# Delta-rule layer of a four-layer decoder trunk: another order of the projection strips, GpSimd splits of the values' weights dropped, and the inverses' matmuls queued behind the third strip of values

## The chip, the cores and the metric

The kernel runs on one core of a Trainium2 chip. The metric is device time in microseconds of one execution. Before the change three runs took 872.19 (median), 870.34 and 872.74 us.

## The reference, cut to what matters

The trunk is four residual layers on 256 tokens of 1024 channels in float32: pooling mixer, gated delta rule, latent attention, pooling mixer again, then a last RMSNorm. The change is in the second layer, the gated delta rule. Of one head (8 heads, keys of 128, values of 256), with `q`, `k`, `v` from a projection, a causal convolution of four taps and SiLU:

```
proj = h @ w_in                                  # 1024 -> q 1024, k 1024, v 2048, gate 2048, b 8, a 8
A    = I + strict_lower((beta k) k^T * decay)    # per chunk of tokens
u, w = A^-1 (beta v),  A^-1 (beta k exp(g))      # a triangular solve
v_new  = u - w state
o      = (q exp(g)) state + lower(q k^T * decay) v_new
state  = state exp(g_last) + (k exp(g_last - g))^T v_new
y = (rmsnorm(o) * silu(gate)) @ w_out            # and x = x + y
```

The reference solves in chunks of 64 tokens; the kernel takes chunks of 128, so there are two chunks (16 triangles of 128 x 128 with the 8 heads) and one step of the recurrence.

## The kernel before, in words

**Split products.** Each float32 weight is split into two float32r parts, `hi` (a ScalarE cast, L117) and `lo` (raw minus hi, L119). A product takes three matmuls: hi by hi, hi by lo, lo by hi. `weights` (L101) loads one unit of two channel tiles of 128 x 512 with one or more DMAs on SyncE's queue into a `raw` buffer, casts each tile on ScalarE and subtracts on VectorE, or on GpSimd where the tile's number is in the argument `pool`. The `raw` buffer is free for the next load once both subtractions have read it.

**Strips.** The layer's projection is done in twelve strips of 512 columns, eight channel tiles each, by `project` (L132). A strip of keys, queries or values is made channel-major: 8 x 4 x 3 = 96 matmuls of 256 columns on L127 to L129 into two PSUM banks of `acc`; then come the convolution (ScalarE L633, VectorE L636), SiLU, transposes on TensorE (keys and queries L675, values L778) and, for values, a scaled copy on ScalarE (L781, tile `vR`). A strip of gates is token-major: 8 x 2 x 3 = 48 matmuls of 512 columns on L167, and two SiLUs on ScalarE (L556).

**The string `order` (L559)** lists the steps: g0 to g3 are gate strips, k and q strips of keys and queries, v0 to v3 values, d and a0, a1 the decays and the triangles (`LT`, L692), s the substitution, i the inverses, u0 and u1 the first chunk's new values.

```
order = "g0 k0 d a0 g1 k1 a1 s q0 v0 i v1 v2 q1 g2 u0 v3 u1 g3".split()   # L559
pool=((0, 4), (7,), (3, 7), (7,))[vi]        # gate, L553
pool=((1, 3, 5, 7), (3, 7), (), ())[vi]      # values, L767
```

**The substitution (s, L712)** inverts the 64 diagonal blocks of 32 x 32 at once, on 64 partitions of GpSimd. SyncE's queue writes the blocks out to DRAM (`d_l`, L718) and reads them back as `Lb` (L721); GpSimd then does 31 rounds of a product (L726, tile `pr`) and a subtraction (L730, tile `Tb`), each waiting for the one before; SyncE's queue writes `Tb` out (`d_t`, L732) and reads it into `T` in eight loads (L736).

**The inverses (i, L787)** grow these blocks to 64 and 128 by products on TensorE: `pairs` (L803, matmuls on L806 and L812) for both chunks, then `whole` (L817, L820, L824, L830). The first matmul of `pairs`, L806, reads `T`. The new values (u0, u1, L847) and all that follows read the inverses, `U`.

**What sets the order of the work.** The program is written in this order, but it is given to a planner (`schedule_with_timeline_sim=True`, L1236) that models the run beforehand and fixes for each engine, and for SyncE's DMA queue, one sequence of instructions. An instruction that is ready in the model goes ahead of those that stand earlier in the program and are not. On the chip each engine follows its sequence strictly: what the model placed early and what is late in fact holds up all that stands behind it on that engine. `later(...)` (L85) adds an order by hand: an instruction made within it comes after the named ones on the same engine. The planner also gives out buffers (`auto_bufs=True`).

Of the kernel before, what the change touches and what calls it, by code (L numbers as in the profile page):

```python
# [18 lines left out]
S = 256  # L19
# [23 lines left out]
def trunk(ctx: ExitStack, tc: tile.TileContext, x, positions, norm_g, pool_w_in, pool_w_grp,  # L43
# [24 lines left out]

# [1 line left out]
    def big(name, *dims, dt=F32):  # L70
# [14 lines left out]
    def later(*instructions):  # L85
        """What an engine gets within it comes after those of these that it gets too."""
        order = ExitStack()
        for ins in instructions:
            order.enter_context(tc.issue_after(ins))
        return order  # L90

    # weights that are ready early are not to be split ahead of a layer's input
    mark = {}
# [3 lines left out]
    def weights(src, n, cols, raw=None, pool=()):  # L97
        """One unit of weights, split into two float32r parts that add up to it."""
        if raw is None:
# [26 lines left out]
    def mm3(o, lhs, rhs, start, stop):  # L126
        nc.tensor.matmul(o, lhsT=lhs[0], rhs=rhs[0], start=start, stop=False)  # L127
        nc.tensor.matmul(o, lhsT=lhs[0], rhs=rhs[1], start=False, stop=False)  # L128
        nc.tensor.matmul(o, lhsT=lhs[1], rhs=rhs[0], start=False, stop=stop)  # L129

    def project(src, ks, act, cols=CW, chan=False, tail=0, done=None, cuts=1,
                where="acc", pool=()):  # L132
        """act (channel-major, split) times a block of columns; src(k0, n) is its weights.

        ks lists the units (first channel tile, how many), in the order to go through them.
        Token-major: one bank per token tile; channel-major: one bank per two
        channel tiles. The last `tail` units go by token tile and by `cuts` parts of the columns,
        each followed by done(t, part, its bank).
        """
        first, last = ks[0][0], sum(ks[-1]) - 1  # L140
# [5 lines left out]
        if chan:  # L146
            banks = [bank(acc if where == "acc" else aux, where) for _ in range(2)]
            for k0, n in ks:
                parts = unit(k0, n)
                for j in range(n):  # L150
                    k = k0 + j
                    for c in range(cols // P):
                        w = [v[:, c * P:(c + 1) * P] for v in parts[j]]
                        o = banks[c // 2][:, (c % 2) * S:(c % 2 + 1) * S]
                        mm3(o, w, act(k, 0, S), k == first and c % 2 == 0,
                            k == last and c % 2 == 1)
            return banks
# [33 lines left out]
    def split_out(*tiles):  # L191
        """Tiles of one bank, each (times a per-partition scale) into two float32r parts."""
        for ps, (hi, lo), scale in tiles:
# [17 lines left out]
    class Split:  # L211
        """Channel-major activations in two float32r parts, four channel tiles to a tile."""

# [18 lines left out]

    # ---- the residual stream. The square sum of a row but its last part goes along with that
    # part, as the square of one more column ----
    xs = [const.tile([P, D + 1], F32, name=f"x{t}") for t in range(NT)]
# [28 lines left out]
    make_identity(nc, ident)  # L264
    # the activation table and TensorE's clock, while the first loads run
    warm = small("warm", 2, bufs=1)
# [14 lines left out]
    class Normed:  # L281
        """The residual over its mean square's root, times a gain. Every other part of a row
        meets the gain before the root is known."""

# [27 lines left out]
    class LayerIn(Normed):  # L312
        """The normed residual of a layer, channel-major, made one token tile at a time."""

# [16 lines left out]
    def cols_of(w, c0, cols=CW):  # L331
        v = w.rearrange("(k p) c -> p k c", p=P)
        return lambda k0, n: v[:, k0:k0 + n, c0:c0 + cols]
# [14 lines left out]
    def layer_out(w, yT, ks, i):  # L348
        """The output projection into the residual, and the start of the next layer."""
        def done(t, a, ps):  # L350
# [20 lines left out]

# [1 line left out]
    place = {}  # L373
# [24 lines left out]
    def window_counts():  # L398
        """w / (t + 1) for the first tokens of the pooling windows."""
        cnt = workb("cnt", 16)  # L400
# [8 lines left out]

    # ================= multi-scale causal pooling =================  # L410
    def pool_layer(i, j, hT):
# [64 lines left out]
        for g in order:  # L476
            gs = gate(g)
            if not place:
                with later(*[m for k, m in mark.items() if k != "rest"]):
                    turn_params()  # L480
                    window_counts()
            elif setups:
                with later(*[m for k, m in mark.items() if k != "rest"]):
                    setups.pop(0)()
# [7 lines left out]

    # ================= gated DeltaNet =================
    GC = {}

    def gdn_setup():
# [15 lines left out]

        # convolution taps, one column per (tap, channel tile)
        crow = workb("crow", P)
# [20 lines left out]
    def gdn_layer(i, j, hT):  # L535
# [15 lines left out]
        def gate(vi):  # L551
            banks = project(cols_of(w_in, 2 * GDN_QK + GDN_V + vi * CW), units(KD), hT,
                            pool=((0, 4), (7,), (3, 7), (7,))[vi])  # L553
            gs.append(big("gsg", NT, CW))
# [3 lines left out]

        order = "g0 k0 d a0 g1 k1 a1 s q0 v0 i v1 v2 q1 g2 u0 v3 u1 g3".split()  # L559
        while order[0][0] == "g":  # L560
            gate(int(order.pop(0)[1]))

        # beta and the log decays
        ps = bank(aux, "aux")
# [36 lines left out]

        # decays: DT[t][j, h, i] = exp(G_i - G_j) for i >= j, and exp(G_i) for the second chunk
        ps = bank(aux, "aux")
# [24 lines left out]
        def conv(*tiles):  # L628
            """Causal depthwise convolution of the channel tiles of a bank."""
            def tp(n, c):  # L630
# [8 lines left out]

        # the substitution's unit diagonals, and room for the inverses  # L640
        Q, B = 4, 32
# [17 lines left out]
        def channels(dst, c0, hf, which):  # L659
            """Four heads of keys or queries, channel-major, and their square sums."""  # L660
            banks = project(cols_of(w_in, c0 + hf * CW), units(KD), hT, chan=True,
# [21 lines left out]
        def against(dst, rhs, sf, hf, t):  # L683
            """Keys against keys or queries of one chunk, decayed and scaled, four heads."""
            ps = bank(aux, "aux").rearrange("p (b s) -> p b s", b=4)
# [26 lines left out]
        def substitution():  # L712
            """Inverses of the unit lower triangles' 32 x 32 diagonal blocks; decayed keys."""
            d_l = dram.tile([M * Q, B * B], F32, name="d_l")
# [46 lines left out]

        # values, token-major, over the keys' inverse norms
        vR = []

        def values(vi):
            banks = project(cols_of(w_in, 2 * GDN_QK + vi * CW), units(KD), hT, chan=True,
                            pool=((1, 3, 5, 7), (3, 7), (), ())[vi])  # L767
            vR.append(big("vR", NT, CW))
# [18 lines left out]
        def inverses():  # L787
            """The blocks below the diagonal ones, by products: 32 to 64, 64 to 128.

            T is lower triangular and U its transpose. Of a product only the columns that  # L790
            the mask keeps are worked out: of two blocks of 32 each time, then of 64.
            """
            U.extend(big("U", H, P) for _ in range(NT))
# [40 lines left out]

            for stage in (pairs, whole):
                for t in range(NT):
                    stage(t)

        def news(hf):
            """The first chunk's new values."""  # L840
            h0 = 4 * hf
# [20 lines left out]

        # the two chunks, head by head
        yT = Split("yT", POOL_W // P)
# [9 lines left out]
        def unseen(h):  # L874
            """The second chunk's values less what the state holds for their keys."""
            ps = bank(aux, "aux")
# [57 lines left out]

    # ================= latent attention =================
    def rope_tables():
        """cos twice, and (-sin, sin), token-major."""
        inv = small("inv", HALF, bufs=1)
# [47 lines left out]
    def mla_layer(i, j, hT):  # L986
# [13 lines left out]
        def rotate(ps, t, nh, o):  # L1000
            """Rotary embedding of nh heads, token-major, from PSUM."""
            def shaped(a):
# [74 lines left out]

        # Products of 256 columns take split operands; the rest whole ones. Of queries and
        # probabilities that parts the token tiles.
        v, qT, kT, qrT = [], [], [], []  # L1080
# [73 lines left out]
        def flipped(h):  # L1154
            """Probabilities, key-major: the first keys for all queries, then the rest."""
            sb = probs.pop(h)
# [90 lines left out]
```

## Time and profile before

| | |
|---|---|
| median of three runs | 872.19 us |
| lowest and highest run | 870.34, 872.74 us |
| span of the profiled execution | 864.8 us |
| median less that span | 7.4 us |
| instructions | 16123 |
| HBM read, written | 137.79 MB, 1.58 MB |

The page of the profile tells of one execution. Its span runs from the first to the last instruction; what lies around it, about 7.4 us of the median, is not in the page. The page has each engine's busy time, then rows of 40 slices of the span (21.6 us each) in which a digit is a busy share in tenths, then the chain of work that ended last, then groups of instructions by line. The trace behind the page answers narrower questions: rows of one engine in order of time, who waited for whom, and busy time by stretch. A row of the timeline reads: start, duration, engine, line, operation, tile written <- tiles read, tile sizes, count, and in brackets the engine's idle time before it with what ended it. PE is TensorE's matmuls, PEld its weight loads, DVE VectorE, ACT ScalarE, POOL GpSimd, SPq SyncE's DMA queue.

The delta-rule layer runs from about 168 to 432 us of the span.

### The profile page before, as it was taken

Reading aid. Unit: us, or ns where it says so; the run is one execution under the profiler, and the core shown is the slowest. Engines: PE = TensorE matmul, PEld = TensorE weight load, DVE = VectorE, ACT = ScalarE, POOL = GpSimd, SP = SyncE. Lnnn points to the kernel's source line nnn. Section 1 sums busy time; section 2 is a strip of 40 time slices with the busy share of each in tenths; the row PEclk is TensorE's granted clock in tenths of the full one; section 3 lists DMA queues with packets and bytes.
Section 4 is the critical chain, followed back from the end, with each engine's and each line's share of the span. In section 5 each row is a group of like instructions: output and inputs, shape, how many; then the busy total and the mean of one; then the engine's idle time right before and its main releaser. Section 6 shows DMA issues by size and latency. Waiting matters only on the chain.

```text
span 864.8 us, 16123 instructions
## 1 busy us (share of the span) xinstructions
PE 843.5 (98%) x5965; PEld 779.9 (90%) x5965; DVE 590.0 (68%) x1138; ACT 488.1 (56%) x1007; POOL 156.6 (18%) x290
## 2 busy tenths in 40 slices
PE   7999999999999979999999999999999999999996
PEld 6999998988999868888989989988978989999986
DVE  5588776466889666466567658767766667867852
ACT  5566655468756535455555645555554566565542
POOL 4010000233258932022202002000000110000012
PEclk8999999999999989999999999999999999999999
DMA  6766656557565463123567676632542547566651
GB/s 211 235 194 185 183 172 219 171 158 228 158 172 168 124 191 102 46 84 137 146 183 221 170 171 194 190 104 75 171 146 59 181 144 207 188 180 191 196 194 50
DMA packets 111288, 140.43 MB, mean 162 GB/s; under 512 B 23340, under 2 KB 53224, under 8 KB 111208
## 3 DMA queue, kind: packets, MB, share of 16 engines
q1 hardware_dynamic: 109056, 138.17, 53.4%
q0 software_dynamic: 320, 1.06, 0.4%
q8 instruction: 47, 0.77, 0.4%
q10 hardware_dynamic: 1832, 0.16, 0.2%
q14 instruction: 33, 0.27, 0.1%
HBM read 137.79 MB, written 1.58 MB: 161 GB/s over the span
## 4 chain that ended last, share of the span: by engine, by line
PE 85%; POOL 7%; DVE 3%; DMA 2%; issue 1%; ACT 1%; SPq 1%; POOLq 0%; ACTq 0%; DVEq 0%
PE acc L167 34%; PE acc L128 11%; PE acc L127 11%; PE acc L129 11%; PE aux L127 2%; POOL Tb L730 2%; PE aux L128 2%; POOL pr L726 2%; PE aux L129 2%; DMA gain<-in_norm_g_dram 1%; PE aux L1134 1%; DVE h L303 1%; DVE wlo L119 1%; PE aux L688 1%; PE tp L1159 1%
## 5 line engine op out<-in xcount | busy, mean ns | idle before, releaser
L119 DVE TENSOR_TENSOR wlo<-raw,whi 128x512 fp32r<-128x512 f32 (+1 forms) x491 | 336.9, 709 | 166.6 <-ACT whi L117 160.1
L117 ACT CAST whi<-raw 128x512 fp32r<-128x512 f32 (+1 forms) x508 | 301.4, 617 | 262.8 <-PE acc L167 92.3
L127 PE MATMUL acc<-hTh,whi 128*128 128x256 f32 x832 | 235.8, 284 | 3.3 <-DVE cv L636 3.3
L128 PE MATMUL acc<-hTl,whi 128*128 128x256 f32 x832 | 236.1, 284 | 0.0
L129 PE MATMUL acc<-hTh,wlo 128*128 128x256 f32 x832 | 235.4, 283 | 0.0
L127 PEld LDWEIGHTS acc<-hTh,whi 128*128 128x128 f32 x832 | 158.2, 190 | 4.2 <-ACT whi L117 3.7
L128 PEld LDWEIGHTS acc<-hTl,whi 128*128 128x128 f32 x832 | 158.3, 190 | 0.4
L129 PEld LDWEIGHTS acc<-hTh,wlo 128*128 128x128 f32 x832 | 158.3, 190 | 0.2
L167 PE MATMUL acc<-whi,yTh 128*128 128x256 f32 (+1 forms) x384 | 116.3, 323 | 0.0
L167 PE MATMUL acc<-wlo,yTh 128*128 128x256 f32 (+1 forms) x384 | 116.2, 319 | 0.0
L167 PE MATMUL acc<-whi,yTl 128*128 128x256 f32 (+1 forms) x384 | 92.4, 321 | 0.0
L167 PEld LDWEIGHTS acc<-whi,yTh 128*128 128x128 f32 x384 | 71.9, 188 | 5.2
L167 PEld LDWEIGHTS acc<-wlo,yTh 128*128 128x128 f32 x384 | 72.0, 188 | 5.1
L167 PEld LDWEIGHTS acc<-whi,yTl 128*128 128x128 f32 x384 | 63.1, 188 | 5.6
L291 POOL TENSOR_TENSOR hg<-x,gain 128x256 f32<-128x256 f32 x18 | 15.4, 860 | 271.7 <-DVE x L353 267.9
L167 PE MATMUL acc<-wlo,hTh 128*128 128x512 f32 (+1 forms) x144 | 56.5, 396 | 0.8 <-DVE wlo L119 0.5
L167 PE MATMUL acc<-whi,hTh 128*128 128x512 f32 (+1 forms) x144 | 55.9, 394 | 0.7 <-ACT hTh L195 0.7
L167 PE MATMUL acc<-whi,hTl 128*128 128x512 f32 (+1 forms) x144 | 45.8, 390 | 0.0
L434 POOL COPY win<-u 128x4 f32<-128x4 f32 x8 | 2.8, 353 | 176.8 <-ACT u L428 176.8
L167 PEld LDWEIGHTS acc<-wlo,hTh 128*128 128x128 f32 x144 | 27.4, 191 | 7.6 <-DVE wlo L119 2.1
L167 PEld LDWEIGHTS acc<-whi,hTh 128*128 128x128 f32 x144 | 27.5, 191 | 6.6 <-ACT hTh L195 1.4
L119 POOL TENSOR_TENSOR wlo<-raw,whi 128x512 fp32r<-128x512 f32 x17 | 23.6, 1389 | 49.4 <-ACT whi L117 49.3
(336 smaller groups left out, 1440.8 us busy)
## 6 DMA issues: line engine op xcount, KB each, us to landing
raw<-in_pool_w_in_dram SPq DMA_DIRECT2D x60, 512.0 KB, 4.5
raw<-in_gdn_w_in_dram SPq DMA_DIRECT2D x48, 512.0 KB, 3.9
raw<-in_pool_w_out_dram SPq DMA_DIRECT2D x32, 512.0 KB, 3.9
raw<-in_mla_w_in_dram SPq DMA_DIRECT2D x24, 512.0 KB, 4.4
raw<-in_mla_w_uq_dram SPq DMA_DIRECT2D x36, 256.0 KB, 3.4
raw<-in_pool_w_grp_dram SPq DMA_DIRECT2D x16, 512.0 KB, 4.0
raw<-in_gdn_w_out_dram SPq DMA_DIRECT2D x16, 512.0 KB, 3.7
raw<-in_mla_w_ukv_dram SPq DMA_DIRECT2D x32, 256.0 KB, 3.2
```

Of the source, the lines that this page charges most:

```text
L117: a = nc.scalar.copy(hi, v)
L119: b = e.tensor_tensor(out=lo, in0=v, in1=hi.bitcast(F32), op=ALU.subtract)
L127: nc.tensor.matmul(o, lhsT=lhs[0], rhs=rhs[0], start=start, stop=False)
L128: nc.tensor.matmul(o, lhsT=lhs[0], rhs=rhs[1], start=False, stop=False)
L129: nc.tensor.matmul(o, lhsT=lhs[1], rhs=rhs[0], start=False, stop=stop)
L167: nc.tensor.matmul(o, lhsT=act(k, t * P, P)[x], rhs=parts[j][z][:, sl], start=k == first and x == z == 0, stop=k == last and x == 1)
L291: nc.gpsimd.tensor_tensor(out=self.early[t, a], in0=xs[t][:, sl], in1=self.g[:, sl], op=ALU.mult)
L303: nc.vector.scalar_tensor_tensor(out=h[:, cut:], in0=xs[t][:, sl], scalar=r[:, 0:1], in1=self.g[:, sl], op0=ALU.mult, op1=ALU.mult)
L688: nc.tensor.matmul(ps[:, b], lhsT=kT[hf][:, b, tt], rhs=rhs[hf][:, b, tt], start=True, stop=True)
L726: nc.gpsimd.tensor_tensor(out=pv, op=ALU.mult, in0=Lb[:, r, r + 1:, None].to_broadcast([M * Q, n, c]), in1=Tb[:, r:r + 1, :c].to_broadcast ...
L730: nc.gpsimd.tensor_tensor(out=tv, in0=tv, in1=pv, op=ALU.subtract)
L1134: nc.tensor.matmul(ps[:, spans[0]], lhsT=r0[bb, pr], rhs=krT[bb], start=False, stop=False)
```

## The change

Four things change; the rest of the diff takes out comments and docstrings.

```diff
@@ gate (L551)
-                            pool=((0, 4), (7,), (3, 7), (7,))[vi])
+                            pool=((0, 4), (7,), (), (7,))[vi])
...
-        order = "g0 k0 d a0 g1 k1 a1 s q0 v0 i v1 v2 q1 g2 u0 v3 u1 g3".split()
+        order = "g0 k0 d a0 g1 k1 a1 s q0 v0 g2 v1 v2 i q1 u0 v3 u1 g3".split()
@@ values (L765)
-            banks = project(cols_of(w_in, 2 * GDN_QK + vi * CW), units(KD), hT, chan=True,
-                            pool=((1, 3, 5, 7), (3, 7), (), ())[vi])
+            banks = project(cols_of(w_in, 2 * GDN_QK + vi * CW), units(KD), hT, chan=True)
@@ inverses (L787)
-            for stage in (pairs, whole):
-                for t in range(NT):
-                    stage(t)
+            with later(mark["pe"]):
+                for stage in (pairs, whole):
+                    for t in range(NT):
+                        stage(t)
@@ mm3 (L126), project (L155)
-        nc.tensor.matmul(o, lhsT=lhs[1], rhs=rhs[0], start=False, stop=stop)
+        return nc.tensor.matmul(o, lhsT=lhs[1], rhs=rhs[0], start=False, stop=stop).ins
...
-                        mm3(o, w, act(k, 0, S), k == first and c % 2 == 0,
-                            k == last and c % 2 == 1)
+                        mark["pe"] = mm3(o, w, act(k, 0, S), k == first and c % 2 == 0,
+                                         k == last and c % 2 == 1)
@@ pool_layer (L479, L483): the new mark is left out of what the setups come after
-                with later(*[m for k, m in mark.items() if k != "rest"]):
+                with later(*[m for k, m in mark.items() if k not in ("rest", "pe")]):
```

First, the third gate strip, g2, moves from behind the second strip of queries to a place ahead of the second strip of values, v1. Second, the inverses' step i moves from behind v0 to behind v2. Third, eight `lo` subtractions go from GpSimd to VectorE: four of v0, two of v1, two of g2. Fourth, the inverses' instructions on TensorE come, in TensorE's sequence, after the last channel-major matmul that stands ahead of them in the program, which is the last of v2. No arithmetic is added or removed.

More of the change, by code (lines that the diff above doesn't have):

```diff
@@ L482, in pool_layer @@
             elif setups:
-                with later(*[m for k, m in mark.items() if k != "rest"]):
+                with later(*[m for k, m in mark.items() if k not in ("rest", "pe")]):
                     setups.pop(0)()
```

## The prediction

> **What bounds the kernel now.** I read the page first, then TensorE in long stretches, then TensorE's waits and rows around the one stretch where it falls behind, then the engine behind that wait.
>
> ```profile
> span 864.8 us, 16123 instructions
> ...
> PE 843.5 (98%) x5965; PEld 779.9 (90%) x5965; DVE 590.0 (68%) x1138; ACT 488.1 (56%) x1007; POOL 156.6 (18%) x290
> ...
> PEclk8999999999999989999999999999999999999999
> ```
>
> TensorE is busy almost throughout, so a change that adds and removes no arithmetic can give back only time in which TensorE waits or is slow. After the start one slice of forty has a clock below full, the fifteenth (303 to 324 us), and it lies in the layer that changes. Busy time by stretch around it:
>
> ```profile
> 228.00:260.00 32.00, 31.62 (x270) 31.37 (x269) 26.81 (x57) 18.05 (x38) 14.13 (x10) 1.00 0.63 175
> 260.00:303.00 43.00, 43.00 (x319) 40.40 (x317) 35.10 (x72) 25.28 (x52) 39.25 (x57) 1.00 0.49 145
> 303.00:317.00 14.00, 8.13 (x43) 7.79 (x42) 8.72 (x16) 4.22 (x8) 7.23 (x13) 0.76 0.58 166
> 317.00:350.00 33.00, 32.96 (x253) 29.60 (x254) 21.49 (x36) 17.56 (x38) 5.31 (x6) 1.00 0.42 132
> ```
>
> The columns are the stretch, its length, the busy time of PE, PEld, DVE, ACT and POOL, the granted clock and DMA. TensorE is full up to 303 us and from 317 us on; between, it does 8.13 us of 14, at a mean clock of 0.76. The waits from 170 to 430 us, then TensorE's rows and the groups from 303 to 317 us:
>
> ```profile
> PE acc L127 <- DVE cv L636: 3.3, 1, 3.3
> PE aux L806 <- DMA T<-d_t: 2.6, 1, 2.6
> PE aux L830 <- DVE X L827: 0.8, 1, 0.8
> ```
>
> ```profile
> 302.54 0.63 PE L167 MATMUL acc<-whi,hTl 128*128 128x512 f32 x2
> 306.44 0.55 PE L127 MATMUL acc<-hTh,whi 128*128 128x256 f32 x1 [3.28 <-DVE cv L636]
> ...
> 312.72 0.28 PE L129 MATMUL acc<-hTh,wlo 128*128 128x256 f32 x1
> ...
> 313.43 0.28 PE L129 MATMUL acc<-hTh,wlo 128*128 128x256 f32 x1
> ...
> 314.13 0.28 PE L129 MATMUL acc<-hTh,wlo 128*128 128x256 f32 x1
> 317.04 1.97 PE L806 MATMUL aux<-T,LT 128*128 128x64 f32 x16 [2.63 <-DMA T<-d_t]
> ```
>
> ```profile
> L127 PE MATMUL acc<-hTh,whi 128*128 128x256 f32 x14 | 5.4, 386 | 3.3 <-DVE cv L636 3.3
> L128 PE MATMUL acc<-hTl,whi 128*128 128x256 f32 x14 | 5.2, 371 | 0.0
> L129 PE MATMUL acc<-hTh,wlo 128*128 128x256 f32 x14 | 5.1, 366 | 0.0
> ```
>
> So g2 ends at 303.17; TensorE waits 3.28 us for a bank that the convolution of q1 still holds; then 42 matmuls of v3 (14 + 14 + 14) take from 306.44 to 314.41, 7.97 us, the first of them slow; then it waits 2.63 us for `T`, and L806 starts the inverses at 317.04. At full clock six matmuls lie between 312.72 and 313.43, 0.118 us each, so the 42 are 4.96 us of work and the slow clock cost 3.0 us. The loss is 3.28 + 3.0 + 2.63 = 8.9 us. That is nearly all that a change of order can win in this stretch, 1.0% of the time.
>
> The next question is which of the three would still be there without the others. The chain of waits runs through GpSimd:
>
> ```profile
> 253.43 2.79 DMA d_l<-LT
> 256.33 3.82 DMA Lb<-d_l
> ...
> 310.87 2.94 DMA d_t<-Tb
> 314.76 2.19 DMA T<-d_t
> ```
>
> ```profile
> 260.22 0.23 POOL L726 TENSOR_TENSOR pr<-Lb,Tb 64x31 f32<-64x31 f32 x1 [1.51 <-DMA Lb<-d_l]
> ...
> 275.41 0.91 POOL L726 TENSOR_TENSOR pr<-Lb,Tb 64x231 f32<-64x231 f32 x1
> ...
> 293.80 1.28 POOL L119 TENSOR_TENSOR wlo<-raw,whi 128x512 fp32r<-128x512 f32 x1
> 295.04 0.58 POOL L726 TENSOR_TENSOR pr<-Lb,Tb 64x231 f32<-64x231 f32 x1
> ...
> 299.47 1.29 POOL L119 TENSOR_TENSOR wlo<-raw,whi 128x512 fp32r<-128x512 f32 x1
> 300.72 1.05 POOL L730 TENSOR_TENSOR Tb<-Tb,pr 64x192 f32<-64x192 f32 x1
> ...
> 310.60 0.25 POOL L730 TENSOR_TENSOR Tb<-Tb,pr 64x31 f32<-64x31 f32 x1
> ```
>
> The substitution runs from 260.22 to 310.85 us without a gap that matters, and with its two DMAs `T` reaches TensorE at 317.04. Had TensorE not waited at 303 us, it would only have come to L806 sooner and waited there. The substitution is the bound of this stretch. TensorE's end is therefore: when `T` arrives, plus all of TensorE's work that its sequence has put behind L806, since after 317 it is full.
>
> From 260.22 to 317.04 are 56.8 us, of which TensorE lost 8.9 and worked 47.9. The planner put L806 where it expected `T`, after 47.9 us of work; so in fact the chip's `T` came 8.9 us later than its plan.
>
> **The change part by part.** *GpSimd's splits.* Two of the eight lie inside the substitution, those of g2 at 293.80 and 299.47: 1.24 us up to 295.04 and 1.25 up to 300.72. Without them `T` comes 2.5 us sooner. The six of v0 and v1 lie ahead of it:
>
> ```profile
> L119 POOL TENSOR_TENSOR wlo<-raw,whi 128x512 fp32r<-128x512 f32 x6 | 9.1, 1510 | 14.3 <-ACT whi L117 14.3
> ```
>
> GpSimd waited 14.3 us among these six and 1.51 us more for `Lb`, so taking them away wins nothing. They go to VectorE:
>
> ```profile
> L119 DVE TENSOR_TENSOR wlo<-raw,whi 128x512 fp32r<-128x512 f32 (+1 forms) x491 | 336.9, 709 | 166.6 <-ACT whi L117 160.1
> ```
>
> At 0.709 us six are 4.3 us, in a stretch (228 to 260) in which VectorE is busy 26.81 of 32 us; it holds them, but `LT`, which the substitution's input waits for, is also made there. I take nothing for it, since a later start that the planner foresees lets TensorE do more ahead of it; unforeseen, up to 1.5 us, about two splits.
>
> *The splits do not leave the substitution alone on VectorE.* The product on 64x231 elements took 0.91 us at 275.41 and 0.58 at 295.04. VectorE's rows say what differs:
>
> ```profile
> L119 DVE TENSOR_TENSOR wlo<-raw,whi 128x512 fp32r<-128x512 f32 x27 | 22.1, 833 | 7.7 <-ACT whi L117 7.7
> ```
>
> ```profile
> 299.62 1.69 DVE L119 TENSOR_TENSOR wlo<-raw,whi 128x512 fp32r<-128x512 f32 x1 [7.04 <-ACT whi L117]
> ```
>
> From 292.6 to 299.6 VectorE stood still, and there the products run short; where it splits, they run 0.33 us longer. From 260 to 311 it made 27 splits. With g2's two it makes 29, and as it will not stand still for 7 us, up to four more: 0.7 to 2.0 us more for GpSimd. I take four splits, 1.3. So `T` moves by -2.5 + 1.3 = -1.2 us (-1.8 to -0.5), to 315.8.
>
> The Trainium skill, "SBUF — State Buffer", Terms, says that VectorE and GpSimd take turns at one shared port pair, and that the one that loses it stands still for the other's whole instruction. The trace agrees in direction (0.91 against 0.58); by that rule four splits of 0.709 us would take 2.8 us back, and the sum below would come out 1.5 us longer.
>
> *The stall on q1's convolution* (3.28 us and the slow clock behind it). Its cause is the load queue:
>
> ```profile
> SPq L104 <- POOL wlo L119: 28.8, 8, 8.6
> ```
>
> Loads waited up to 8.6 us for a `raw` buffer that a GpSimd split, queued behind the substitution, had not read; the 7.04 us of VectorE above are the same wait seen from its end, and q1's convolution was queued behind it. With the splits on VectorE and g2, which has no convolution, ahead of v1, this stall goes. What is late next is `T`: TensorE reaches L806 sooner and waits there. Alone this wins nothing.
>
> *The place of the inverses in TensorE's sequence.* Before the change L806 already stands behind v0, v1, v2, q1, g2 and 42 of 96 matmuls of v3. The strips ahead of it are the same set in the new order, so the order by hand behind v2 binds nothing. But the planner also counts on `T` coming earlier, by about the 2.5 us of the two splits; then L806 stands 2.5 us of work (21 matmuls) further ahead, and that work comes after `T`. That is +2.5 us (0 if the place does not move; a later place is the first rival).
>
> *The clock.* TensorE now has one wait instead of two: 56.8 - 1.2 - (47.9 - 2.5) = 10.2 us. Before, the slow 42 matmuls lay ahead of a wait for `T`, in its shadow; behind L806 nothing shadows them, and v3's matmuls, with which the inverses alternate, are full work. The nearest row is the stall of 3.28 us, whose aftermath cost 3.0; the wait of 2.63 cost nothing. A wait of 10.2 us is nearer the first, and I take 2.5 us (0 to 3.0).
>
> The Trainium skill, "TensorE: Matmul & The Clock Gate", Part 1, says that the array falls to half clock after an idle window of about 3.4 us and comes back after a busy one. The trace agrees (0.76 granted in 303 to 317 us); an estimate from that page is 1.7 to 3.4 us, which would leave the sum where it is.
>
> *The 0.8 us at L830* and the rest of the layer I leave as they are: their work and order do not change.
>
> Sum: -1.2 + 2.5 + 2.5 = +3.8 us: a span of 868.6 in place of 864.8. The median, 872.19, has 7.4 us beside that span; I move it by the same amount, to **876.0**. The ends: -1.8 + 0 + 0 = -1.8 (870.4), and -0.5 + 2.5 + 3.0 + 1.5 = +6.5 (878.7).
>
> **The rivals.** *First: the inverses fall later in TensorE's sequence (faster).* If all of v3 stands ahead of L806, its other 54 matmuls, 6.4 us, are done while `T` is on its way; TensorE gets there at 260.2 + 47.9 + 6.4 = 314.5, waits 1.3 us and keeps its clock: -1.2 - 6.4 = -7.6 us, 864.6. With part of g3 ahead too, the whole 8.9 us go: 863.3. It beats the forecast from the point at which some 20 matmuls more than before stand ahead. For it:
>
> ```profile
> 284.55 0.60 PE L778 MATMUL tp<-ident,vc 128*128 128x128 f32 x4
> ```
>
> ```profile
> 317.24 1.56 ACT L781 ACTIVATE vR<-tp,rki 128x256 f32<-128x256 f32 x4
> ```
>
> v1 was transposed by 285 us and copied out only at 317.24, beside the inverses' start: with i ahead of v1 in the program its tiles were granted behind the inverses'. With i behind v2 that knot is untied, and TensorE may run further before the planner's `T`. Against it: what places L806 is the substitution, and that gets shorter in the plan. Chance 0.28.
>
> *Second: the parts cancel (no change).* L806 keeps its place and the slow clock costs about 1.2 us: 0.0, 872.2. Chance 0.24.
>
> *Third: the order by hand does bind,* the planner expecting `T` so early that L806 stands right behind v2. Then q1 (96 matmuls) and 42 of v3, 138 x 0.118 = 16.3 us, come after `T`: -1.2 + 16.3 + 2.5 = +17.6, 889.8. Against it: before, it expected `T` a whole strip and a half later. Chance 0.07.
>
> *That the change does not do what it says* is so for the order by hand in my forecast already.
>
> **How the numbers follow.** The measurement tells about 0.3%, 2.6 us, from no change. My forecast, +3.8 us, has 0.41; with the third rival slower has 0.48, the same 0.24, faster 0.28. The forecast's own range is 870.4 to 878.7. For 8 in 10 it must reach to the first rival's 864.6: 864.0 to 879.0; left out are the third and the first's last microseconds.
>
> **What would show it.** Right: one wait of about 10 us of L806 for `T` with no stall on `cv` before it; fewer than 42 matmuls of v3 ahead of L806; no GpSimd row of L119 within the substitution, which ends about 1 us sooner after its start; a granted clock of one half just behind L806. Wrong: all of v3 ahead of L806 and no wait over 3 us (first rival), or L806 ahead of q1 (third). It is also wrong if TensorE is not full after L806, for then work moved behind it costs nothing.

## The result and the profile after

After the change twelve runs took 875.12 us (median; 872.12 to 877.44), twelve of the kernel before, beside them, 871.00 (868.08 to 872.74). The ratio is 1.0054 [1.0036, 1.0071]: slower by 4.1 us, with a forecast of +3.8. As will be seen, the sum came out right with some terms that were wrong.

The profiled execution of before, on which the prediction was built, was among its quickest. Over all executions the time is 1.7 us above the span, not 7.4, so that one took 866.6 us, 4.4 under the median, and its granted clock over the whole span was 0.991, where the mean of 87 runs of this kernel is 0.987.

The page of after:

```profile
span 872.5 us, 16110 instructions
...
PE 846.5 (97%) x5965; PEld 780.2 (89%) x5965; DVE 593.5 (68%) x1146; ACT 488.3 (56%) x1007; POOL 145.8 (17%) x282
...
PEclk9999999999999979999999999999999999999999
```

Eight instructions have left GpSimd (290 to 282) and eight have come to VectorE (1138 to 1146). The dip of the clock is in the fifteenth slice, as before, and deeper (7 for 8). TensorE's waits from 165 to 440 us:

```profile
PE aux L805 <- DMA T<-d_t: 7.0, 1, 7.0
PE acc L127 <- DVE vc L636: 1.6, 1, 1.6
PE aux L829 <- DVE X L826: 0.8, 1, 0.8
```

L805 is before's L806. The 3.3 us for `cv` are gone and the wait for `T` has grown from 2.6 to 7.0 us. The same stretches as before:

```profile
260.00:303.00 43.00, 41.40 (x336) 40.39 (x335) 37.69 (x73) 28.01 (x58) 38.65 (x53) 1.00 0.56 175
303.00:317.00 14.00, 7.04 (x56) 6.86 (x54) 4.26 (x7) 6.05 (x14) 6.42 (x17) 0.79 0.33 81
317.00:350.00 33.00, 33.00 (x237) 29.63 (x237) 23.55 (x44) 13.43 (x27) 4.86 (x6) 0.94 0.41 130
```

From 317 us on TensorE is full in both, but its clock, 1.00 before, is 0.94: 237 matmuls fit where there were 253. Three rows show the chain, GpSimd's first and last round of the substitution and L805:

```profile
262.11 0.79 POOL L726 TENSOR_TENSOR pr<-Lb,Tb 64x31 f32<-64x31 f32 x1 [0.45 <-DMA Lb<-d_l]
```

```profile
309.72 0.24 POOL L730 TENSOR_TENSOR Tb<-Tb,pr 64x31 f32<-64x31 f32 x1
```

```profile
315.68 3.65 PE L805 MATMUL aux<-T,LT 128*128 128x64 f32 x16 [6.96 <-DMA T<-d_t]
```

The substitution starts 1.9 us later in the span than before, ends 0.9 us sooner and takes 47.9 us instead of 50.6. The first sixteen matmuls of the inverses take 3.65 us; before, they took 1.97. That is the slow clock.

A loss that the prediction did not have lies 380 us further on, where the third layer (latent attention) hands over to the last. TensorE's two longest waits from 680 to 720 us, then the longest one before:

```profile
PE tp L323 <- ACT h L308: 2.0, 1, 2.0
PE acc L167 <- DVE x L353: 0.8, 1, 0.8
```

```profile
PE acc L167 <- DVE wlo L119: 0.5, 1, 0.5
```

VectorE there, first after, then before:

```profile
696.79 0.69 DVE L119 TENSOR_TENSOR wlo<-raw,whi 128x512 fp32r<-128x512 f32 x1 [1.72 <-ACT whi L117]
697.40 1.08 DVE L353 TENSOR_TENSOR x<-acc,x 128x256 f32<-128x256 f32 x3
```

```profile
689.70 0.42 DVE L353 TENSOR_TENSOR x<-acc,x 128x256 f32<-128x256 f32 x1 [0.27 <-PE acc L167]
691.81 0.43 DVE L353 TENSOR_TENSOR x<-acc,x 128x256 f32<-128x256 f32 x1 [1.68 <-PE acc L167]
```

L353 is the residual addition that the next layer's input needs. Before, it waits for TensorE, as it should. After, three are done in a row, behind a split of the last layer's weights that itself waited 1.72 us for ScalarE's cast, which waited for its load. No line of that code was edited. The planner's sequences for the third layer and for this boundary are others than before. Counted from its first transpose on L323 to that of the next layer, the third layer took 268.8 us before and takes 271.8; the delta-rule layer, counted the same way, took 252.9 and takes 256.4; the last layer, to the end of the span, took 169.0 and takes 171.0, with 3.4 us at half clock from 703.5 us on.

### The profile page after: what moved, and what is told of

Same layout as the page of the kernel before. It is cut to its first block, busy times and chain, and to the rows that moved or that the text cites. A ratio compares the mean times of both kernels' runs of the same rounds, so it can differ in the third digit from the quotient of the medians.

```text
span 872.5 us, 16110 instructions
## 1 busy us (share of the span) xinstructions
PE 846.5 (97%) x5965; PEld 780.2 (89%) x5965; DVE 593.5 (68%) x1146; ACT 488.3 (56%) x1007; POOL 145.8 (17%) x282
## 4 chain that ended last, share of the span: by engine, by line
PE 82%; POOL 7%; DMA 4%; DVE 4%; issue 2%; ACT 1%; SPq 0%; POOLq 0%; ACTq 0%; DVEq 0%
PE acc L167 32%; PE acc L128 11%; PE acc L127 11%; PE acc L129 11%; POOL Tb L730 3%; PE aux L127 2%; POOL pr L726 2%; PE aux L128 2%; PE aux L129 2%; DMA raw<-in_pool_w_in_dram 1%; DVE wlo L119 1%; PE aux L1135 1%; DMA Gb<-d_g 1%; PE aux L805 1%; PE tp L1160 1%
## 5 line engine op out<-in xcount | busy, mean ns | idle before, releaser
L119 DVE TENSOR_TENSOR wlo<-raw,whi 128x512 fp32r<-128x512 f32 (+1 forms) x499 | 342.0, 708 | 165.3 <-ACT whi L117 157.2
L167 PEld LDWEIGHTS acc<-whi,hTl 128*128 128x128 f32 x144 | 26.9, 192 | 5.7 <-DVE hTl L200 0.3
```

The costliest lines, as they stand in the source:

```text
L119: b = e.tensor_tensor(out=lo, in0=v, in1=hi.bitcast(F32), op=ALU.subtract)
L167: nc.tensor.matmul(o, lhsT=act(k, t * P, P)[x], rhs=parts[j][z][:, sl], start=k == first and x == z == 0, stop=k == last and x == 1)
```

## The experiments

**Order and pools apart.** The first kernel has the new `order` alone, the second the splits on VectorE alone; neither has the order by hand.

```diff
 order_only (against before)
-  ... s q0 v0 i v1 v2 q1 g2 u0 v3 u1 g3
+  ... s q0 v0 g2 v1 v2 i q1 u0 v3 u1 g3
 pools_only (against before)
-  gate pool=((0, 4), (7,), (3, 7), (7,))   values pool=((1, 3, 5, 7), (3, 7), (), ())
+  gate pool=((0, 4), (7,), (), (7,))       values without pool
```

> The new order of the strips alone, with the old GpSimd splits and no order by hand. In TensorE's sequence the inverses' first matmul stands behind 31 matmuls of v3 (42 before the change, 30 after it). My theory (the end is T's arrival plus what the sequence has put behind the inverses): two GpSimd splits, now v1's, still lie in the substitution, which takes about 50 us as before, so T comes as before; 11 matmuls fewer stand ahead of it, +1.3 us, and the slow clock now falls behind the wait, +2.7 us: 3 to 5 us slower than before, 1.0035 to 1.006. Rival A, the loss comes from the eight splits that moved to VectorE: without them the time is that of before, within 1 us (0.999 to 1.001). Rival B, the loss comes from the replanned rest of the program (the boundary to the last layer, 3 us in the profile after): the delta-rule layer's own length is that of before, 252.9 us.

> The old order, with the splits of v0, v1 and g2 moved from GpSimd to VectorE, no order by hand. In TensorE's sequence 60 matmuls of v3 stand ahead of the inverses (42 before). My theory: T comes about 1 us sooner after the substitution's start, 18 matmuls more (2.1 us) are done ahead of it, and the slow clock behind the wait costs 2.7 us: within 1.5 us of before (0.9985 to 1.002). Rival A, VectorE's extra splits are the loss: 4 us or more slower, as after the change (1.004 to 1.007). Rival B, the replanned rest: the layer's own length as before, 252.9 us, whatever the total.

Measured: the order alone 1.0008 [0.9992, 1.0025], the pools alone 1.0005 [0.9990, 1.0020]. Neither half is slower, which my theory had wrong for the order and rival A for the pools: the loss needs both halves. Rival B asked for a delta-rule layer of 252.9 us; it took 257.0 and 259.2, but before's own second profile, further down, has 258.1, so that sign decides nothing. What rival B says of the end holds: the third layer takes 268.8 us in both halves, as before. The waits of TensorE in the layer, order alone, then pools alone:

```profile
PE aux L806 <- DMA T<-d_t: 4.4, 1, 4.4
PE tp L778 <- ACT vc L774: 3.0, 1, 3.0
```

```profile
PE aux L805 <- DMA T<-d_t: 11.9, 1, 11.9
```

The wait for `T` differs by 7.5 us and the time does not. With the pools alone 60 matmuls of v3 stand ahead of L805 (31 with the order alone), and the substitution starts 5.1 us later than before, counted from the end of the `bws` matmuls. What is done before a wait is not left for behind it.

**All of v3 ahead of the inverses,** the prediction's first rival made by hand.

```diff
-  ... g2 v1 v2 i q1 u0 v3 u1 g3
+  ... g2 v1 v2 q1 v3 i u0 u1 g3
```

> The changed kernel with the inverses behind the fourth strip of values in the order, and by hand behind its last matmul: all 96 matmuls of v3 stand ahead, 66 more than after the change. My theory: TensorE gets to the inverses 7.8 us later, at about the time T arrives; the wait of 7.0 us and the slow clock of 2.7 us go: 7 to 10 us faster than after the change, 3 to 5 us faster than before, 0.994 to 0.997 of it. Rival A (VectorE's load is the loss): as after the change, 1.004 to 1.007. Rival C (the work behind the inverses is bound by their own chain, not by TensorE, once v3 is gone from it): the wait goes and returns as gaps between L805 and L829, 0 to 3 us gained on after, 1.002 to 1.006.

Measured 1.0052 [1.0030, 1.0074], which is in the ranges of rivals A and C. TensorE's longest waits in the layer, and ScalarE:

```profile
PE tp L675 <- ACT kqT L669: 6.1, 2, 5.9
PE aux L829 <- DVE X L826: 1.6, 2, 0.8
PE aux L823 <- ACT T L820: 1.3, 2, 0.7
PE aux L811 <- DVE X L807: 0.9, 1, 0.9
```

```profile
301.65 0.82 ACT L633 ACTIVATE cv<-acc,tap 128x256 f32<-128x256 f32 x2
309.76 0.84 ACT L780 ACTIVATE vR<-tp,rki 128x256 f32<-128x256 f32 x2 [7.29 <-POOL pr L726]
```

The wait for `T` is gone. The last three lines are rival C's gaps, 3.8 us where after has 0.8; the first line no theory had: a wait on the same substitution has taken the place of the wait for `T`. A tile `vR` has a buffer that the substitution has to give back, ScalarE stands 7.29 us at its copy with q1's work queued behind, and TensorE waits for q1. Behind the inverses only g3 is left, and the clock is at half from 345.4 us for 17.1 us.

**One part for five strips.** For g2, v1, v2, q1 and v3 no `lo` part is worked out; `hi` stands in its place, so all matmuls are still there, but the result lacks the low part of these weights and counts the product with their high part twice.

```diff
+  if lo is None:          # g2, v1, v2, q1, v3
+      parts.append((hi, hi))
+      continue
```

> The changed kernel in which the weights of g2, v1, v2, q1 and v3 have no low part: the low part's subtraction is left out and its product takes the high part again, so VectorE makes no split while the substitution runs; every matmul is still there. 29 matmuls of v3 stand ahead of the inverses (30 after the change). My theory: VectorE's splits stand in GpSimd's way by about 0.3 us each, so the substitution falls from 47.9 us to about 40, T comes about 8 us sooner, the wait of 7.0 us and the slow clock go: 8 to 10 us faster than after the change, 0.993 to 0.996 of before. Rival D (GpSimd's steps take what they take, and the planner is simply wrong on them): the substitution stays at 46 to 48 us and the time at that of after, 1.004 to 1.007.

Measured 0.9841 [0.9816, 0.9866], 14 us under before and 18 under after, where my theory had 8 to 10 under after. In the profiles 12.9 us of it are in the delta-rule layer; 3.0 and 2.3 are in the third and the last, since this kernel has before's sequences there (268.8 and 168.7 us). The groups of GpSimd around the substitution, after the change, then here (seven lines further down in the code):

```profile
L730 POOL TENSOR_TENSOR Tb<-Tb,pr 64x31 f32<-64x31 f32 (+15 forms) x31 | 21.6, 698 | 2.4
L726 POOL TENSOR_TENSOR pr<-Lb,Tb 64x31 f32<-64x31 f32 (+15 forms) x31 | 19.5, 628 | 2.6 <-DMA Lb<-d_l 0.5
```

```profile
L737 POOL TENSOR_TENSOR Tb<-Tb,pr 64x31 f32<-64x31 f32 (+15 forms) x31 | 16.7, 537 | 2.3
L733 POOL TENSOR_TENSOR pr<-Lb,Tb 64x31 f32<-64x31 f32 (+15 forms) x31 | 15.0, 483 | 4.2 <-DMA Lb<-d_l 2.0
```

The same 62 instructions are 9.4 us shorter without VectorE's splits beside them (41.1 to 31.7): the contention that the prediction read from two rows. After, 27 splits run within the substitution, so one costs GpSimd 0.35 us in the mean; the prediction had 0.33. And the stretch in which TensorE waits for `T` before and after the change:

```profile
303.00:317.00 14.00, 14.00 (x127) 14.00 (x125) 12.01 (x22) 7.59 (x16) 0.17 (x1) 1.00 0.53 148
```

TensorE is full, at full clock. With no wait over 0.8 us in the layer there is no half clock at all between the start and the end.

**Both kernels again,** for a second profile of each.

> The kernel before, unchanged, for a second profile. Its shown profile (span 864.8 us) is about 4.5 us shorter than its median. Theory L (the whole 4 to 5 us between the kernels is lost in the delta-rule layer, as the prediction's sum has it): the layer takes 252 to 254 us again and the rest of its span is what varies. Theory R (much of the loss comes from a re-planned end: the planner wrote another sequence for the third layer and for the boundary to the last one, 3.0 and 2.0 us longer in the profile after): the layer takes 255 to 258 us, near the 256.4 us after, and the third layer takes 268.8 and the rest 169.0 us again.

> The kernel after, unchanged, for a second profile. Theory R: the third layer is again about 3 us longer than before's (271 to 272 us against 268.8), with the wait of L323 for ScalarE's h of about 2 us at the boundary and a slice of half clock behind it, and the last part again about 171 against 169 us. Theory L: these 5 us are noise of one execution; third layer 268.8 to 269.5, last part about 169, and the delta-rule layer is 257 us or more.

Theory R's in the main. The third layer took 268.8 us before and 272.2 after, as in the first profiles (268.8, 271.8); but the last took 169.0 and 169.6, not 171, for after's half clock of 3.4 us there did not come back. Before's delta-rule layer took 258.1 us this time (252.9 in the first profile), after's 260.0 (256.4). The waits of before again, and L806:

```profile
PE aux L806 <- DMA T<-d_t: 5.5, 1, 5.5
PE acc L127 <- DVE cv L636: 3.3, 1, 3.3
```

```profile
317.06 3.65 PE L806 MATMUL aux<-T,LT 128*128 128x64 f32 x16 [5.52 <-DMA T<-d_t]
```

L806 starts where it did (317.04 and 317.06). Only the clock differs: in the first profile the half clock came at 305.8 us for 6.8 us, all in the shadow of the wait for `T`; in the second it came at 314.9 for 10.2 and at 355.8 for 3.4 us, and all but its first 2.2 us fell on work that nothing shadows. The stretch from 317 to 330 us in both profiles of before, then in both of after:

```profile
317.00:330.00 13.00, 12.96 (x121) 12.96 (x121) 8.73 (x12) 8.69 (x21) 1.29 (x2) 1.00 0.56 172
```

```profile
317.00:330.00 13.00, 12.94 (x85) 12.97 (x86) 6.91 (x9) 6.85 (x18) 1.27 (x1) 0.69 0.42 130
```

```profile
317.00:330.00 13.00, 13.00 (x101) 13.00 (x102) 10.64 (x20) 4.10 (x9) 1.27 (x1) 0.84 0.54 167
```

```profile
317.00:330.00 13.00, 13.00 (x92) 13.00 (x92) 11.00 (x19) 3.95 (x8) 0.96 (x1) 0.75 0.57 170
```

So one and the same program does 121 or 85 matmuls in 13 us. The slow clock behind L806 is no mark of the change; it is a draw that both kernels make. The boundary's loss, on the other hand, is there again in the second profile of after:

```profile
PE tp L323 <- ACT h L308: 2.1, 1, 2.1
PE acc L167 <- DVE x L353: 0.9, 1, 0.9
```

**Fewer splits ahead of the last layer's input.** Here the delta-rule layer's sequence is that of after, and only the boundary changes.

```diff
-  held_back.update(free=FREE, after=ins)                        # FREE = 4
+  held_back.update(free=2 if self.i == 3 else FREE, after=ins)  # free2; 1 in free1
```

> The kernel after, but at the boundary from the third to the last layer two of the next layer's weight splits are let ahead of its first input tile in place of four, so that no split waits for its load ahead of the residual additions. The delta-rule layer keeps its sequence. Theory R: the boundary loss goes, 3 to 5 us: 870 to 872 us, 0.998 to 1.002 of before. Theory L: the loss lies in the delta-rule layer, so this changes under 1 us: 1.004 to 1.006 of before. Between (3 us of wait, the slow clock behind it staying): 1.002.

> As the run with two splits let ahead of the first input tile of the last layer, now with one (the layer's own sequence is that of after). Where two were let ahead, 1.1 us of TensorE waiting for a split were left at the boundary, and the time was 1.0026 of before. Theory R (all the loss is at the boundary): the rest goes too, 0.999 to 1.001 of before. Theory M (mixed: the boundary carried some 3 us, the other 1.5 to 2 us of the loss are the delta-rule layer's: 12 matmuls of v3 behind L805 and the slow clock there): 1.0015 to 1.003, the boundary's waits under 1 us and the delta-rule layer 257 to 260 us.

Measured 1.0026 [1.0005, 1.0047] with two, nearest the 1.002 named for the case between the theories, and 1.0068 [1.0042, 1.0094] with one, outside both of its theories. In both the two waits of the boundary are gone; what is there instead is, in both:

```profile
PE acc L167 <- DVE wlo L119: 1.4, 2, 1.1
```

By the median two splits win 2.65 us and one loses 1.9, which no theory allowed for. The clock explains most of the difference. Each run has its granted clock; (1 - clock) x span is the most that the slow clock can have cost (its deficit). Where half clock falls into a wait it costs nothing: over the 87 runs of before the time rises by 0.72 ± 0.06 us for each us of deficit, so the column of time less deficit takes off too much where the deficit is large (1.7 us for behind_v3 against before). Means over each kernel's runs, with standard errors:

| | runs | deficit, us | time less deficit, us | end of the program |
|---|---|---|---|---|
| before | 87 | 11.5 ± 0.2 | 859.6 ± 0.2 | before's |
| after | 13 | 12.5 ± 0.7 | 862.8 ± 0.5 | after's |
| free2 | 12 | 10.8 ± 0.5 | 862.4 ± 0.3 | after's, mended |
| free1 | 7 | 14.9 ± 0.8 | 862.0 ± 0.4 | after's, mended |
| order_only | 11 | 11.9 ± 0.6 | 859.1 ± 0.5 | before's |
| pools_only | 11 | 11.6 ± 0.5 | 860.1 ± 0.3 | before's |
| i_behind_q1 | 12 | 13.8 ± 0.2 | 859.0 ± 0.3 | before's |
| v0_back | 12 | 11.8 ± 0.2 | 859.4 ± 0.3 | before's |
| behind_v3 | 8 | 17.5 ± 0.6 | 857.8 ± 0.3 | before's |
| s_early | 12 | 12.9 ± 0.3 | 860.8 ± 0.3 | before's |
| s_early_g2_last | 10 | 14.7 ± 0.3 | 860.6 ± 0.3 | before's |

At 0.72 us for each us of deficit, after stands 3.5 ± 0.4 us above before, free2 2.6, free1 3.4, and behind_v3 level with it. The two mended kernels gain 0.4 and 0.8 us on after in time less deficit, no more than the errors. Their profiles show more: the third layer takes 270.0 and 269.8 us, 1.8 to 2.4 less than after's, and still 1.0 to 1.2 more than before's, about the wait shown. The last layer takes 169.8 and 172.2, the second with 3.4 us at half clock; TensorE's idle time in it is 8.2 and 8.9 us, where after has 8.0 and 8.1 and before 7.6.

**The inverses' step one place later,** and then the same with v0's four splits back on GpSimd.

```diff
 i_behind_q1 (against after)
-  ... v1 v2 i q1 u0 v3 u1 g3
+  ... v1 v2 q1 i u0 v3 u1 g3
 v0_back: that, and
+  values pool=((1, 3, 5, 7), (), (), ())
```

> The kernel after with the inverses' step one place later in the string (v2 q1 i). In its sequence 43 matmuls of v3 stand ahead of L806's place (after 30, before 42), all splits of values and g2 stay on VectorE, and the end (third layer, boundary) has before's sequence. Theory L: only the place changes, 13 matmuls x 0.118 = 1.5 us gained of the 4.7: 1.0030 to 1.0045 of before, delta-rule layer about 1.5 us shorter than after's. Theory R: that and the end: 1.5 + 3 to 5 us gained: 0.997 to 1.001. A third theory S (the later start of the substitution, 2.7 us in the profile after, is what the layer loses, since the splits of v0 and v1 delay LT): as theory L, with the substitution starting at 262 to 264 us.

> The kernel with i one place later (v2 q1 i), and the four splits of v0, which lie ahead of the substitution, back on GpSimd as before the change; those of v1 and g2 stay on VectorE, and no GpSimd split falls within the substitution. Third layer and boundary as before. Theory S (v0's splits on VectorE delay LT and so the substitution's start): it starts 69.5 to 70.5 us behind the end of the bws matmuls (71.9 in the run with i one place later, 70.0 before), takes 47.5 to 48.5 us, the inverses start 2 to 3 us sooner than there, and the time is 0.998 to 1.000 of before. Rival C (VectorE's work only moves: what GpSimd gives back before the start comes back as contention or as a wait on kqT): the inverses start less than 1 us sooner, 1.001 to 1.003.

Measured 1.0019 [1.0004, 1.0035] and 1.0002 [0.9984, 1.0021]. The first falls between theories L and R: 3.8 us better than after in time less deficit, with a deficit 1.3 us larger. Its delta-rule layer has all of after's splits, and with this one shift the planner writes before's end again: the third layer takes 268.8 us. Theory S's sign, a start of the substitution at 262 to 264 us, is there too (262.1). In the second the substitution started 68.8 us behind the `bws` matmuls (71.9 in the first), so theory S is right that v0's splits delay it, though it took 49.6 us instead of 47.9. The inverses came no sooner (129.1 us behind the `bws` matmuls, 127.7 in the first), as rival C says, and the time lies between the ranges of the two: TensorE met the buffers first. The waits of the first, then of the second:

```profile
PE tp L675 <- ACT kqT L669: 5.4, 1, 5.4
PE aux L805 <- DMA T<-d_t: 2.5, 1, 2.5
```

```profile
PE acc L127 <- ACT vR L781: 6.5, 1, 6.5
```

**The substitution earlier,** by g1 behind s, a try at a faster version. The second kernel also has g2 behind the inverses.

```diff
 s_early (against after)
+  g0 k0 d a0 k1 a1 s g1 q0 v0 g2 v1 v2 q1 i u0 v3 u1 g3
 s_early_g2_last
+  g0 k0 d a0 k1 a1 s g1 q0 v0 v1 v2 q1 v3 i g2 u0 u1 g3
```

> The kernel after with the gate strip g1 moved from ahead of k1 to behind s, and the inverses' step one place later (v2 q1 i): the substitution can start a strip of gates (about 11 us of TensorE) earlier against the strips, while in TensorE's sequence 45 matmuls of v3 stand ahead of L806's place (after 30). Third layer and boundary have before's sequence. Theory W (what the layer loses in both kernels is the wait for T, and the half clock that follows a wait): T is there before TensorE is, no wait over 1.5 us, no half clock between 300 and 360 us, delta-rule layer 244 to 249 us, 0.988 to 0.994 of before. Rival K (the keys' chain to LT on VectorE and ScalarE, not the strip, sets the start of the substitution; it starts at 256 us or later and the wait stays): 0.998 to 1.003. Rival B (buffers given out against the substitution's end stop ScalarE and so TensorE, as where all of v3 stood ahead): a wait of 5 us or more on kqT or vR, 0.997 to 1.005.

> The kernel after with g1 behind s, all of v3 ahead of the inverses and g2 behind them (s g1 q0 v0 v1 v2 q1 v3 i g2 u0 u1 g3): against the kernel before 54 matmuls of 256 columns more and 48 of 512 columns fewer ahead of L806, about 5 us less work; two gate strips are left to fill the gaps between the inverses' steps. Theory W: T about 11 us earlier, TensorE some 5 us earlier than before, wait under 2 us, no gaps between the inverses' steps, 0.988 to 0.994 of before. Rival K: the substitution starts at 256 us or later, TensorE waits 5 us or more for T: 0.999 to 1.006. Rival B: a wait of 5 us or more on kqT or vR: 0.997 to 1.005.

Measured 1.0030 [1.0012, 1.0048] and 1.0045 [1.0027, 1.0064]. The substitution started at 259.8 and 259.2 us, not at 249, which is rival K's start; its wait for `T` did not come, for TensorE waited elsewhere first. k1's matmuls were done by 214 us in the first of these, its `LT` only at 246 to 248; so the keys' chain on the other engines, not the strip on TensorE, sets the start. Rival B's wait came, and both times are in its range; the first kernel, then the second:

```profile
PE tp L675 <- ACT kqT L669: 6.3, 2, 5.4
```

```profile
PE tp L675 <- ACT kqT L669: 7.5, 2, 6.6
```

No kernel that computes the whole reference was found faster than before.

## Why the prediction was right, and where it was not

**The bound was right.** The end of the layer is when `T` arrives, plus what stands behind L806, plus the clock. The stall on `cv` went, as forecast, and won nothing; the wait for `T` grew instead. It was 7.0 and 5.2 us, not 10.2, since TensorE had a new wait of 1.6 us, and less of v3 moved than forecast.

**T's arrival: -1.2 forecast, -0.5 and -0.9 measured** (end of the `bws` matmuls to L806: 126.8 and 126.6 us before, 126.3 and 125.8 after). Two errors nearly cancelled. The prediction let the later start of the substitution cost nothing, or 1.5 us at most; it is 2.7 and 2.9 us later. And it let four more VectorE splits fall into the substitution, +1.3; 27 fell in before and 27 and 26 after, so the substitution is 2.8 and 3.1 us shorter instead of 1.2. Its end therefore hardly moved. Of the gain that was measured, 0.5 and 0.7 us lie in the two DMAs behind it (6.2 and 6.3 us before, 5.7 and 5.6 after), which the prediction took as fixed. That v0's splits make the start late is shown by the run that moves them back.

**The place of the inverses: +2.5 forecast, +1.4.** 30 matmuls of v3 stand ahead of L805, where 21 were forecast and 42 stood before: 12 x 0.118 us. The profiles bear it out: from the inverses' first matmul to the end of the layer, less half of the time at half clock, before takes 110.0 and 109.6 us, after 111.2 and 111.0, and free2 and free1, which have after's place, 111.0 each. In the other kernels this count is off by up to 1.3 us; order_only, with 31 matmuls ahead, takes 110.1.

**The clock: +2.5 forecast as new.** This step failed. There were 5.6 us at half clock behind L805 in the first profile of after, worth 2.8 us, as forecast, and 7.4 and 6.8 us in the second, worth 7.1; but in the second profile of before there were 8.1 and 3.4 us, worth 5.7. The prediction took the one execution that had its slow clock in the shadow for the rule. Over all runs the deficit differs by 1.0 ± 0.7 us, worth 0.7 at 0.72 us for each.

**The order by hand** binds nothing, as forecast: without `later(mark["pe"])` the planner writes the same sequence for every engine.

**What was missing** is the end of the program. The prediction ended its sum where the diff ends. The third layer takes 268.8 to 268.9 us in all ten profiles of kernels with before's end and 271.8 and 272.2 in the two of after: +3.0 and +3.4, of which 2.8 and 3.0 are the new waits at the boundary. The layer's own terms are -0.7 + 1.4 = +0.7. With 0.3 to 0.5 in the last layer beside its half clock, and the clock's 0.7, that is +4.7 to +5.3; 4.1 was measured (3.1 to 6.2 by the interval of the ratio). In time less deficit after is 3.2 ± 0.5 us above before; all kernels of the table with before's end lie at 857.8 to 860.8, the three with after's at 862.0 to 862.8. So the median of 876.0 was near 875.1 by luck in part: two terms of the sum, the clock and the place, were too high by about what the boundary cost.

**The first rival** (0.28, faster) did not come about by itself, and made by hand it was right on the work behind the inverses alone: with all of v3 ahead, that takes 102.7 us less half of the half clock, 7 under before. But the inverses start 135.8 us behind the `bws` matmuls, 9 us later than before. The rival fell to what its entry did not price: a buffer that the substitution holds, the inverses' bare chain, and a clock deficit 6.0 us larger.

The 3 us are thus placed at the boundary. What stays open is why the two kernels that removed its waits won so little in the time: their third layer is 1.8 to 2.4 us shorter, but the last one is no shorter than after's. Why the planner turns to the other end with a shift of one step is not known.

## What to carry to other kernels

Before a sum is made against a profile, compare that execution's own time and granted clock with the spread of the runs; a stall that is hidden in one profile is paid in the next. When a planner orders the whole program, an edit in one layer can re-order layers that it does not touch, so look at the sequences of all of them before the loss is sought in the edited lines. And a wait that is moved off one tile is only gone if no buffer is waiting for the same producer.

## What the runs showed of the hardware

One VectorE split lengthens GpSimd's work beside it by 0.35 us, half of its own 0.7 us, in the mean over 27 of them. By the Trainium skill, "SBUF — State Buffer", Terms, the one that loses the shared port pair stands still while the other's instruction holds it. The measurement is about half of an instruction; whether each loser waited for all of it or for what was left of it is not shown.

The half clock came in stretches of 3.4, 6.8, 10.2, 13.7 and 17.1 us, multiples of one window. In thirteen of the fourteen profiles a stretch began 2.1 to 5.0 us after the start of a wait of 3.0 to 11.9 us; one_part, without such a wait, has none there. In two profiles (after_again, free1) one also followed a lone wait of 1.8 us. A second stretch, of 3.4 to 10.2 us, came at 353 to 358 us in nine profiles, 37 to 48 us behind the start of the first, where the longest wait was 0.8 us. The Trainium skill, "TensorE: Matmul & The Clock Gate", Part 1, has such a window, of about 3.4 us; the trace agrees with its length. That page has the half clock follow an idle window; here waits much shorter than the window were enough, and the measurement decides. In the second profile of one and the same kernel the half clock came 9 us later than in the first, and the layer took 5.2 us more. That is more than the change did.
